# Four of eight conditioning shifts summed along rows on VectorE instead of multiplied on TensorE

## The chip, the cores and the metric

The kernel runs on one core of a Trainium2 chip, as one launch. The metric is the device time of that launch in microseconds (us). A core has a matrix engine (TensorE, PE in the profile; PEld is its weight load), a vector engine (VectorE, DVE), an activation engine (ScalarE, ACT), GpSimd (POOL) and SyncE (SP), which here only issues transfers. Each engine works through its own queue in order. DMA transfers are issued from SP's queue (nearly all) and from ScalarE's.

## The reference

Two layers of a diffusion backbone over 256 latent tokens and 256 context tokens, 2048 channels wide. Layer 0 is attention plus a state-space mixer, layer 1 a gated short convolution. What matters here is how layer 0 gets its input: a conditioning vector makes a shift, a scale and a gate, and the normalised tokens are scaled and shifted by them, the latent ones with `c`, the context ones with `c_ctx`.

```python
def adaln(cond, w, b):
    m = jax.nn.silu(cond) @ w + b
    return jnp.split(m, 3, axis=-1)

def modulate(h, shift, scale):
    return h * (1 + scale) + shift

shift, scale, gate = adaln(c, ada_w[i], ada_b[i])
h = modulate(rms_norm(x, norm_g[i]), shift[:, None], scale[:, None])
shift_c, scale_c, gate_c = adaln(c_ctx, ada_w[i], ada_b[i])
hc = modulate(rms_norm(ctx, norm_g[i]), shift_c, scale_c)
p = h @ w_in                    # w_in: 2048 x 14400
pc = hc @ w_in[:, base:]
```

`ada_w[0]` is 2048 x 6144 in fp32: 16 MB each for shift, scale and gate. Every weight is read once, and it meets two condition vectors (shift and scale) or one (gate).

## The kernel before

**The schedule.** The kernel is written out by a planner. `Plan` holds a clock for each engine, a table of when each piece of a tile is written, and a clock for the DMA engines, which advances by bytes over `RATE` (270 GB/s). Work besides the main loop sits in generators ("tasks") in three lists, `urgent`, `side` and `back`. A task yields what its next step needs: an engine and tiles, or a condition. `pump` runs every step that by the planner's clocks would find its engine and its tiles ready within a horizon (4500 ns for `urgent`, 2500 for `side`, 1500 for `back`, `HOR`), so the clocks decide the order of instructions on each engine's queue. `force(ok, qs)` runs the best step of the lists `qs` again and again until `ok` holds; the main loop calls it before it writes work that needs a result.

**Loads.** `loads` is one list of transfers in a fixed order, most of them 512 KB in a buffer of 128 x 1024 fp32. There are nine such buffers in this stage (`raw` 0 to 4, and four tiles used later, which the profile shows as `PT`, `xtm` and `yi`). `issue` (L381, L383) takes the next transfer whenever a buffer is free; a user gives its buffer back with `give_raw`. A weight is split into a high and a low part, a cast on ScalarE (L420) and a subtraction on VectorE (L427), into one of three places, and every product is made of three: high by high, high by low, low by high.

**Layer 0's first stage** goes over the 2048 channels in eight blocks j of 256. For each block and each of four token tiles `kv` multiplies with the key and the value weights, for two tiles with the query weights, and `b_part` makes a part of the B projection. Key and value parts of a block go to a bank each and are added up by VectorE (`part_gen`, L789), which frees the bank. A block needs its modulated tokens, split into `hH` and `hL`. The main loop says so:

```python
for j in range(8):
    need[0] = j
    force(lambda: ("h", j, 0 if j == 0 else 3) in got, (urgent,))
```

They come from `ada_gen`, one task that takes the blocks in order. For a block it makes the scale `A0` (part 0), then the shift `S0` (part 1), each from four loads of `ada0`: 16 products of 128 x 32 with the padded condition vectors `cpad` as weights, a copy on ScalarE (L724), two transposes, a short reduction on VectorE (L732) and one or two short additions (L735 to L738). Then for each of the two channel blocks of 128 it computes `hH` on ScalarE (L757, two activations), the same in full fp32 on VectorE (L759, two operations), and the difference `hL` on VectorE (L763). The load order is, for block j: its key and value weights, scale and shift loads of block j+1 (`q_ada`), its query weights, its B weights.

**The gate** of layer 0 and all of layer 1's conditioning are computed by `gemv_gen` in the list `back`: the SiLU of `c` is written to memory as a row (`crow`, by `rows_out`), half a row is loaded to all partitions (`csb`), and each load of transposed weights is multiplied by it and summed along the row in one VectorE operation (L823). Nothing needs these before the output projection of layer 0. In the first stage it runs beside the last blocks.

Of the kernel before, what the change touches and what calls it, by code (L numbers as in the profile page):

```python
# [14 lines left out]
D = 2048  # L15
KB = 16
# [125 lines left out]
def kernel(ctx: ExitStack, tc, x, cx, ada0, w0, adaT, w_in, w_out, sc_in, sc_out, rpb, small, const,  # L142
# [216 lines left out]
    onload = {}  # L359

    later = deque()
    started = [False]
    ngem = [0]

# [120 lines left out]
    def q_ada(j, *parts):  # L485
        for part in range(2):
            if parts and part not in parts:
                continue
            for q in range(4):
                loads.append(("a", ("ada", j, part, q), ada0, 8 * j + 4 * part + q, 4, 0, 256, 2))  # L490

    def q_proj(w, c0, nc_, rows=D):
        room[0] = 2 if w is w_in and c0 >= COL_K else 1
# [208 lines left out]
    def ada_gen():  # L702
        bc = lambda ap: ap.unsqueeze(2).to_broadcast([128, 2, 2])
        for j in range(8):
            k2 = slice(2 * j, 2 * j + 2)
            for part, dst in ((0, A0), (1, S0)):
                ps = None
                for q in range(4):
                    key = ("ada", j, part, q)
# [31 lines left out]
            for ts in ((0, 1), (2,), (3,)) if j == 0 else ((0, 1, 2, 3),):  # L741
                yield when(lambda: all(("xm", t, j) in got for t in ts))
                spans = [(k, slice(max(256 * k, 128 * ts[0]), min(256 * k + 256, 128 * ts[-1] + 128)))
                         for k in range(2) if {2 * k, 2 * k + 1} & set(ts)]
                o = slice(128 * ts[0], 128 * ts[-1] + 128)
                for kb in (2 * j, 2 * j + 1):
                    if j:

                        yield when(lambda: need[0] >= j or plan.t["DVE"] <= plan.t["PE"] + 600)
                    yield W_("DVE", xnT[kb][:, o])  # L750
                    hf = tmp()
                    if hH[kb] is None:
                        hH[kb] = st([128, 512], f"hH{kb}", F32R, name=f"hH{kb}")
                    if ts == (0, 1):
                        split_half(kb)
                    for k, ok_ in spans:
                        E(S.activation(hH[kb][:, ok_], xnT[kb][:, ok_], AF.Identity, scale=A0[:, kb, k:k + 1],  # L757
                                       bias=S0[:, kb, k:k + 1]))
                        E(V.tensor_scalar(out=hf[:, ok_], in0=xnT[kb][:, ok_], scalar1=A0[:, kb, k:k + 1],  # L759
                                          scalar2=S0[:, kb, k:k + 1], op0=ALU.mult, op1=ALU.add))  # L760
# [30 lines left out]
        got.add(("part", j, key, t))  # L791


    mrow, crow = drt([2, D], "mrow"), drt([1, D], "crow")
# [6 lines left out]
    def rows_out(col, dst):  # L801

        yield W_("PE", col, nb=1)
        ps = bank()
        turn(ps[:16, :128], col)
        yield W_("DVE", ps)
        E(V.tensor_copy(rowt[:16, :], ps[:16, :128]))
        give(free_b, ps)
        yield W_("AQ", rowt)
        E(DMA2.dma_start(dst.rearrange("(b c) -> b c", c=128), rowt[:16, :]))  # L810

    def gemv_gen():
        yield from rows_out(csil[:, 0:KB], crow[0])
        for q, blocks in enumerate(GEM):
            for h in range(2):
                yield W_("SP", crow, csb)
# [12 lines left out]
            if q == 1:  # L829
                a, b = p2(16, 32)  # L830
                o = M1.rearrange("p r b -> p (r b)")
                E(V.tensor_tensor(out=o, in0=a, in1=b, op=ALU.add))
                E(V.tensor_tensor(out=o, in0=o, in1=P_("ab1")[:, 0:32], op=ALU.add))
            else:
                a, b = p2(0 if q == 0 else 48, 16)
                E(V.tensor_tensor(out=a, in0=a, in1=b, op=ALU.add))
                E(V.tensor_tensor(out=a, in0=a, in1=P_("ab0" if q == 0 else "ab1")[:, 32:48], op=ALU.add))
                yield from rows_out(a, mrow[q // 2])
            n_back[0] = (3, 11.5, 15)[q]

    spawn(back, gemv_gen())
# [27 lines left out]

    for j in range(8):  # L870
        need[0] = j
        force(lambda: ("h", j, 0 if j == 0 else 3) in got, (urgent,))
        if j == 0:

            w3 = [use(k) for k in range(3)]
# [27 lines left out]
        else:  # L903
# [1209 lines left out]
```

## Time and profile before

| | |
|---|---|
| median of 3 runs | 1753.41 us (1752.1 to 1754.06) |
| the profiled execution, its own time | 1752.57 us |
| its span, first to last instruction | 1750.8 us |
| busy: TensorE, VectorE, ScalarE | 1730.9, 1218.1, 768.5 us |
| first stage, blocks 1 to 7 | 51.4 to 194 us of the span |

The profile is of one execution. A window or timeline counts from the first instruction. Busy times of one engine can overlap by some hundredths of a microsecond at the ends of instructions. "L427" is line 427 of the kernel; helpers record many operations on one line (L195 is every product, L199 every transpose). After `<-` stands what ended an idle time.

### The profile page before, as it was taken

The page shows a single profiled execution, that of the slowest core. Times are in us where ns is not written, and L with a number is a line of the kernel's source. Part 1 is how long each engine was busy: PE and PEld are TensorE (multiplying, and loading weights), DVE is VectorE, ACT ScalarE, POOL GpSimd, SP SyncE. Part 2 cuts the span into 40 slices and gives each one's busy share as a digit, 9 for nine tenths or more (in the row PEclk, how much of TensorE's full clock was granted, in tenths as well). Part 3 has the DMA queues.
Part 4 walks back from the last instruction along what each step waited for, and adds up shares of the span by engine and source line. Part 5 has one row for each costly group of instructions (what it writes and reads, how often), then busy time and mean ns, then how long its engine had stood idle before and what let it go on. Part 6 is the DMA issues. An engine that isn't in the chain of part 4 may idle for free.

```text
span 1750.8 us, 25076 instructions
## 1 busy us (share of the span) xinstructions
PE 1730.9 (99%) x9451; PEld 1461.3 (83%) x9451; DVE 1218.1 (70%) x2042; ACT 768.5 (44%) x1330; POOL 33.2 (2%) x28
## 2 busy tenths in 40 slices
PE   6999999999999999999999999999999999999998
PEld 4777988889888889888888898888888888888887
DVE  5666787868575877675877687887568766555554
ACT  5333544446243435243435243655445444444432
POOL 0000100001000000000001000000000000000000
PEclk9999999999999999999999999999999999999999
DMA  9987644776655766665766667867867878666563
GB/s 368 345 303 259 192 144 121 207 230 203 218 175 150 220 212 183 203 190 163 221 217 183 185 196 248 261 213 260 279 206 253 266 239 257 188 192 193 192 211 114
DMA packets 193369, 378.98 MB, mean 216 GB/s; under 512 B 18096, under 2 KB 57824, under 8 KB 193248
## 3 DMA queue, kind: packets, MB, share of 16 engines
q1 hardware_dynamic: 185984, 370.80, 66.2%
q10 hardware_dynamic: 7264, 6.58, 1.2%
q8 instruction: 74, 1.21, 0.3%
q14 instruction: 47, 0.39, 0.1%
HBM read 369.83 MB, written 7.50 MB: 216 GB/s over the span
## 4 chain that ended last, share of the span: by engine, by line
PE 98%; DMA 0%; DVE 0%; SPq 0%; ACT 0%; issue 0%; POOL 0%; DVEq 0%; ACTq 0%
PE bank L195 95%; PE bank L199 3%; DMA raw<-in_ada 0%; SPq L583 0%; DVE w L427 0%; DVE tmp L603 0%; DVE tmp L759 0%; ACT half L724 0%; ACT x L613 0%; DVE tmp L2016 0%; DVE tmp L2018 0%; DVE hL L763 0%; SPq L381 0%; ACT hH L757 0%; DVE gt L789 0%
## 5 line engine op out<-in xcount | busy, mean ns | idle before, releaser
L427 DVE TENSOR_TENSOR w<-raw,w 128x1024 fp32r<-128x1024 f32 x343 | 416.4, 1217 | 260.6 <-ACT w L420 254.7
L420 ACT CAST w<-raw 128x1024 fp32r<-128x1024 f32 x343 | 359.2, 1049 | 531.2 <-PE bank L195 454.5
L195 PE MATMUL bank<-hH,w 128*128 128x256 f32 (+1 forms) x2064 | 486.5, 324 | 0.0
L195 PE MATMUL bank<-w,hH 128*128 128x512 f32 x1280 | 406.5, 396 | 2.7 <-ACT hH L757 2.5
L195 PEld LDWEIGHTS bank<-hH,w 128*128 128x128 f32 x2064 | 344.7, 188 | 32.0 <-issue 1.7
L195 PE MATMUL bank<-hL,w 128*128 128x256 f32 (+1 forms) x1040 | 334.5, 322 | 0.0
L195 PEld LDWEIGHTS bank<-w,hH 128*128 128x128 f32 x1280 | 236.8, 188 | 54.1 <-issue 4.2
L195 PE MATMUL bank<-w,hL 128*128 128x512 f32 x640 | 249.4, 390 | 0.1
L195 PEld LDWEIGHTS bank<-hL,w 128*128 128x128 f32 x1040 | 196.3, 189 | 14.4
L195 PE MATMUL bank<-w,h 128*128 128x512 f32 x768 | 179.7, 390 | 0.0
L195 PEld LDWEIGHTS bank<-w,h 128*128 128x128 f32 x768 | 143.6, 188 | 29.6
L823 DVE CUSTOM_DVE_ANT_0 raw<-raw,csb 128x1024 f32<-128x1024 f32 x128 | 155.2, 1218 | 11.9 <-DMA raw<-in_adaT 10.0
L195 PEld LDWEIGHTS bank<-w,hL 128*128 128x128 f32 x640 | 120.1, 188 | 25.4 <-DVE hL L763 0.6
L195 PE MATMUL bank<-w,mix 128*128 128x512 f32 x588 | 139.1, 392 | 0.0
L195 PEld LDWEIGHTS bank<-w,mix 128*128 128x128 f32 x588 | 109.1, 188 | 22.4 <-DVE w L427 0.3
L1279 DVE SCALAR_TENSOR_TENSOR tmp<-bank,cwh,tmp 128x508 f32<-128x508 f32 (+1 forms) x96 | 71.1, 745 | 1.9
L195 PE MATMUL bank<-KL,h 128*128 128x512 f32 x264 | 63.9, 389 | 0.0
L427 DVE TENSOR_TENSOR QL<-raw,QT 128x1024 fp32r<-128x1024 f32 x32 | 39.2, 1224 | 29.0 <-ACT QT L420 28.9
L427 DVE TENSOR_TENSOR KL<-raw,KL 128x1024 fp32r<-128x1024 f32 x32 | 39.2, 1224 | 28.4 <-ACT KL L420 28.3
L195 PEld LDWEIGHTS bank<-KL,h 128*128 128x128 f32 x264 | 49.5, 188 | 10.3
L427 DVE TENSOR_TENSOR wL<-raw,wH 128x1024 fp32r<-128x1024 f32 x31 | 37.9, 1224 | 27.4 <-ACT wH L420 27.4
L195 PE MATMUL bank<-QT,h 128*128 128x512 f32 x168 | 56.2, 391 | 0.0
(293 smaller groups left out, 1975.0 us busy)
## 6 DMA issues: line engine op xcount, KB each, us to landing
raw<-in_w_in SPq DMA_DIRECT2D x196, 512.0 KB, 3.8
raw<-in_adaT SPq DMA_DIRECT2D x128, 512.0 KB, 4.7
raw<-in_sc_in SPq DMA_DIRECT2D x128, 512.0 KB, 3.9
raw<-in_w_out SPq DMA_DIRECT2D x64, 512.0 KB, 5.2
raw<-in_ada SPq DMA_DIRECT2D x34, 512.0 KB, 6.8
raw<-in_sc_out SPq DMA_DIRECT2D x32, 512.0 KB, 3.6
PT<-in_ada SPq DMA_DIRECT2D x16, 512.0 KB, 6.9
raw<-in_w SPq DMA_DIRECT2D x16, 512.0 KB, 6.5
```

Of the source, the lines that this page charges most:

```text
L195: E(T.matmul(o, l, r, start=start, stop=stop, skip_group_check=True))
L199: E(T.transpose(o, i, ident if k == 128 else ident[:k, :k]))
L420: E(S.copy(H, v))
L427: E(V.tensor_tensor(out=Lo, in0=v, in1=H.bitcast(F32), op=ALU.subtract))
L823: E(V.tensor_tensor_reduce(out=raw, in0=raw, in1=csb, scale=1.0, scalar=0.0, op0=ALU.mult, op1=ALU.add, accum_out=gp[:, h, m:m + 1]))
L1279: E(V.scalar_tensor_tensor(out=do, in0=di, scalar=cwh[:, 32 * k + ch:32 * k + ch + 1], in1=do, op0=ALU.mult, op1=ALU.add))
```

## The change

For blocks 4 to 7 (`DOTS`) the shift is not multiplied on TensorE. The weights of these shifts are laid out transposed by the host, so that an output channel is a partition and 1024 of the 2048 inputs are a row; the number and size of the loads stay. Both conditions are written to memory as rows (`crow` has two), and a new task `dot_gen` in the list `side` loads each whole row to all 128 partitions, into the tiles `KT` and `KL`, which are free once the tokens are transposed. For every load it issues two VectorE operations that multiply by a condition row and sum along it, one for each condition, then the short reduction and the addition of the bias. `ada_gen` skips the shift of these blocks and waits for it instead. The main loop forces `side` tasks as well as `urgent` ones from block 1 on.

These loads stand beside the scale loads of the same block, two ahead of them and two behind, in the stretch of the load order that belongs to the block before.

The full-fp32 modulated tokens of blocks 1 to 7 are computed on ScalarE (two more activations behind L757's) instead of VectorE. `gemv_gen` starts its loads of `csb` after the last of the new sums, which use `csb` for results that nobody reads. From block 1 to the end of the stage the planner's DMA clock runs at 360 GB/s instead of 270.

```diff
+    DOTS = (4, 5, 6, 7)
@@ q_ada
             for q in range(4):
-                loads.append(("a", ("ada", j, part, q), ada0, 8 * j + 4 * part + q, 4, 0, 256, 2))
+                if part and j in DOTS:
+                    loads.append(("a", ("dot", j, q), ada0, 8 * j + 4 + q, 1, 0, 1024, 2))
+                else:
+                    loads.append(("a", ("ada", j, part, q), ada0, 8 * j + 4 * part + q, 4, 0, 256, 2))
@@ the order of loads
+    dots = deque()
+
+    def dot_load():
+        for _ in range(2):
+            if dots:
+                loads.append(dots.popleft())
+
     for j in range(1, 8):
+        for jj in DOTS:
+            if j == max(1, jj - 1):
+                q_ada(jj, 1)
+                for _ in range(4):
+                    dots.append(loads.pop())
+                dots = deque(sorted(dots, key=lambda a: a[1][1:]))
         w_seg(j, CK, CV)
+        dot_load()
         if j < 7:
-            q_ada(j + 1)
+            q_ada(j + 1, *((0,) if j + 1 in DOTS else (0, 1)))
+        dot_load()
         w_seg(j, CQ)
         weight(w_in, j * 256, 2, COL_B, 256)
@@ ada_gen
             for part, dst in ((0, A0), (1, S0)):
+                if part and j in DOTS:
+                    yield when(lambda: ("S", j) in got)
+                    continue
...
-                    yield W_("DVE", xnT[kb][:, o])
+                    yield W_("ACT" if j else "DVE", xnT[kb][:, o])
...
+                        if j:
+                            E(S.activation(hf[:, ok_], xnT[kb][:, ok_], AF.Identity, scale=A0[:, kb, k:k + 1],
+                                           bias=S0[:, kb, k:k + 1]))
+                            continue
                         E(V.tensor_scalar(out=hf[:, ok_], in0=xnT[kb][:, ok_], scalar1=A0[:, kb, k:k + 1],
                                           scalar2=S0[:, kb, k:k + 1], op0=ALU.mult, op1=ALU.add))
+                    if j:
+                        yield W_("DVE", hf)
@@ the new task
+    def dot_gen():
+
+        yield when(lambda: "crow" in got and all(("xm", t, 7) in got for t in (2, 3)) and need[0] >= 2)
+        full = []
+        for c in range(2):
+            yield W_("SP", crow)
+            full.append(st([128, D], ("KT", "KL")[c], name=f"full{c}"))
+            E(DMA.dma_start(full[c], crow[c].partition_broadcast(128)))
+        part_ = statk.rearrange("p (b c h) -> p b c h", b=4, c=2)
+        for j in DOTS:
+            for q in range(4):
+                yield when(lambda: ("dot", j, q) in RAW)
+                raw = RAW["dot", j, q][0]
+                for c, o in enumerate((csb, raw)):
+                    yield W_("DVE", raw, full[c])
+                    E(V.tensor_tensor_reduce(out=o, in0=raw, in1=full[c][:, (q % 2) * 1024:(q % 2) * 1024 + 1024], scale=1.0,
+                                             scalar=0.0, op0=ALU.mult, op1=ALU.add,
+                                             accum_out=part_[:, q // 2, c, q % 2:q % 2 + 1]))
+                RAW.pop(("dot", j, q))
+                give_raw(raw)
+                issue()
+            k2 = slice(2 * j, 2 * j + 2)
+            yield W_("DVE", statk)
+            S_ = S0[:, k2, :]
+            E(V.tensor_reduce(out=S_, in_=part_[:, 0:2], axis=AX.X, op=ALU.add))
+            E(V.tensor_tensor(out=S_, in0=S_, in1=P_("ab0")[:, k2].unsqueeze(2).to_broadcast([128, 2, 2]), op=ALU.add))
+            got.add(("S", j))
@@ gemv_gen
-        yield from rows_out(csil[:, 0:KB], crow[0])
+        yield from rows_out(csil, crow.rearrange("r (b c) -> (r b) c", c=128), 32)
+        got.add("crow")
+        yield when(lambda: ("S", DOTS[-1]) in got)
@@ the main loop
     spawn(urgent, x_gen(1), 1)
+    spawn(side, dot_gen())
...
         need[0] = j
-        force(lambda: ("h", j, 0 if j == 0 else 3) in got, (urgent,))
+        if j == 1:
+            plan.RATE = 360.0
+        force(lambda: ("h", j, 0 if j == 0 else 3) in got, (urgent,) if j == 0 else (urgent, side))
...
     force(lambda: all(("part", 7, key, t) in got for key in "KV" for t in range(4)), (urgent,))
+    plan.RATE = Plan.RATE
@@ on the host
+    for j in (4, 5, 6, 7):
+        for q in range(4):
+            k0, c0 = (q % 2) * 1024, j * 256 + (q // 2) * 128
+            ada0[8 * j + 4 + q] = f('ada_w')[0][k0:k0 + 1024, c0:c0 + 128].T
```

More of the change, by code (lines that the diff above doesn't have):

```diff
@@ L791, in part_gen @@
         got.add(("part", j, key, t))
-    mrow, crow = drt([2, D], "mrow"), drt([1, D], "crow")
+    mrow, crow = drt([2, D], "mrow"), drt([2, D], "crow")
     M1 = st([128, 2, KB], "M1")
@@ L799, with rows_out @@
     n_back = [0]
-    def rows_out(col, dst):
+    def rows_out(col, dst, n=16):
         yield W_("PE", col, nb=1)
         ps = bank()
-        turn(ps[:16, :128], col)
+        turn(ps[:n, :128], col)
         yield W_("DVE", ps)
-        E(V.tensor_copy(rowt[:16, :], ps[:16, :128]))
+        E(V.tensor_copy(rowt[:n, :], ps[:n, :128]))
         give(free_b, ps)
         yield W_("AQ", rowt)
-        E(DMA2.dma_start(dst.rearrange("(b c) -> b c", c=128), rowt[:16, :]))
+        E(DMA2.dma_start(dst, rowt[:n, :]))
+    in_rows = lambda r: r.rearrange("(b c) -> b c", c=128)
+    def dot_gen():
[24 more added lines that the diff above has]
+            got.add(("S", j))
     def gemv_gen():
-        yield from rows_out(csil[:, 0:KB], crow[0])
+        yield from rows_out(csil, crow.rearrange("r (b c) -> (r b) c", c=128), 32)
+        got.add("crow")
+        yield when(lambda: ("S", DOTS[-1]) in got)
         for q, blocks in enumerate(GEM):
@@ L837, in gemv_gen @@
                 E(V.tensor_tensor(out=a, in0=a, in1=P_("ab0" if q == 0 else "ab1")[:, 32:48], op=ALU.add))
-                yield from rows_out(a, mrow[q // 2])
+                yield from rows_out(a, in_rows(mrow[q // 2]))
             n_back[0] = (3, 11.5, 15)[q]
```

## The prediction

> **What bounds the kernel now.** I read the page first, for what the span is made of.
>
> ```profile
> span 1750.8 us, 25076 instructions
> PE 1730.9 (99%) x9451; PEld 1461.3 (83%) x9451; DVE 1218.1 (70%) x2042; ACT 768.5 (44%) x1330; POOL 33.2 (2%) x28
> PE 98%; DMA 0%; DVE 0%; SPq 0%; ACT 0%; issue 0%; POOL 0%; DVEq 0%; ACTq 0%
> ```
>
> TensorE is busy for 1730.9 of 1750.8 us, and the chain that ended last is TensorE for 98%. So time leaves this kernel only where TensorE gets less to do, and it comes back wherever TensorE is made to wait. The profiled execution took 1752.57 us, 1.77 more than its span; the median of the runs, 1753.41, is 0.84 above that.
>
> Next the windows, cut at the borders of layer 0's first stage. Block 1 starts at 51.4 us, block 2 at 72.3, block 7 at 177.7; its rows end at 194. The columns are the window, its length, busy us (count) of PE, weight load, DVE, ACT and POOL, granted clock, DMA share, GB/s.
>
> ```profile
> 0.00:44.00 44.00, 29.10 (x235) 19.36 (x236) 24.86 (x75) 26.03 (x59) 3.19 (x10) 1.00 0.95 368
> 44.00:51.40 7.40, 7.40 (x40) 5.83 (x38) 6.45 (x15) 6.58 (x15) 0.00 (x0) 1.00 1.03 416
> 51.40:72.30 20.90, 20.90 (x142) 15.77 (x142) 13.13 (x24) 6.62 (x11) 0.00 (x0) 1.00 0.96 355
> 72.30:177.70 105.40, 105.22 (x702) 77.83 (x701) 65.48 (x120) 32.25 (x51) 0.00 (x0) 1.00 0.76 276
> 177.70:194.00 16.30, 16.30 (x73) 13.51 (x72) 11.87 (x17) 3.76 (x5) 0.00 (x0) 1.00 0.50 161
> 194.00:1750.80 1556.80, 1551.95 (x8267) 1328.98 (x8265) 1096.33 (x1795) 693.29 (x1194) 29.99 (x18) 1.00 0.66 206
> ```
>
> From 44 to 194 us TensorE loses 0.18 us in all, with the clock full. VectorE is 62% busy (65.48 of 105.40) where the change puts its sums, ScalarE 31%. The DMA engines are full up to 72 us and then 0.76.
>
> **What is taken from TensorE.** The shift of one block is 16 products, whose 32 records stand as one piece in the timeline, and two transposes. Start, length, engine, operation, tiles, count:
>
> ```profile
> 59.52 0.39 PE L195 MATMUL bank<-w,hH 128*128 128x512 f32 x1
> 59.84 1.93 PE L195 MATMUL bank<-raw,cpad 128*32 128x256 f32 x32
> 61.70 0.50 PE L195 MATMUL bank<-w,hH 128*128 128x512 f32 x1
> 62.04 0.40 PE L195 MATMUL bank<-w,hL 128*128 128x512 f32 x1
> 62.27 0.39 PE L195 MATMUL bank<-w,hH 128*128 128x512 f32 x1
> 62.50 0.38 PE L199 MATMUL bank<-const,half 128*128 128x128 f32 x2
> 62.64 0.48 PE L195 MATMUL bank<-w,hH 128*128 128x512 f32 x1
> 62.95 0.40 PE L195 MATMUL bank<-w,hL 128*128 128x512 f32 x1
> ```
>
> Undisturbed row products start 0.23 us apart (62.04 to 62.27). From the start at 59.52 to that at 62.95 are 3.43 us, in which five row products start; at 0.23 they take 1.15. So one shift costs 2.28 us, the slow starts behind each change of tile shape included. Four shifts are 9.1 us, and no wait covers them, so all of it is on the path: **minus 9.1**.
>
> **What VectorE gets.** Operations by shape between 72.3 and 177.7 us, and three starts in a row:
>
> ```profile
> L427 DVE TENSOR_TENSOR w<-raw,w 128x1024 fp32r<-128x1024 f32 x10 | 12.2, 1223 | 3.5 <-ACT w L420 3.4
> L759 DVE TENSOR_SCALAR tmp<-xm,A,S 128x256 f32<-128x256 f32 x21 | 7.7, 406 | 0.0
> L823 DVE CUSTOM_DVE_ANT_0 raw<-raw,csb 128x1024 f32<-128x1024 f32 x2 | 2.4, 1216 | 0.0
> 169.90 1.22 DVE L823 CUSTOM_DVE_ANT_0 raw<-raw,csb 128x1024 f32<-128x1024 f32 x1
> 171.04 0.08 DVE L823 DVE_READ_ACCUMULATOR2_ANT gp<- 128x1 f32 x1
> 171.04 1.27 DVE L789 TENSOR_TENSOR Vt<-Vt,bank 128x512 f32<-128x512 f32 x2
> ```
>
> The trace has the added operation itself: L823 is the same sum along a row, 1.216 us, with 1.14 to the next start, so its accumulator read costs nothing more. The change adds 4 blocks by 4 loads by 2 sums, 32 of them: 38.9 us by duration, 36.5 by starts. It takes away the L759 group (7.7 us), which goes to ScalarE; the short reductions and additions behind each shift stay as many. Between 72.3 us and block 7, VectorE then has 65.5 − 7.7 + 38.9 = 96.7 us of busy time in 105.4 − 9.1 = 96.3. Busy times overlap by 0.08 each (169.90 + 1.22 against 171.04); over some 131 instructions that is 10, so the need is between 86 and 97 us: 90 to 100%. Nor can the sums begin at 72.3: they wait for the two whole condition rows and a first load, 12 to 16 us by the transfers and landings below; I take 14. In the 82 us left, the rest of VectorE's work is 57.8 × 82/96.3 = 49, together 88 by durations and 79 by starts. Behind a late sum on VectorE's queue stand the additions that free banks and the low halves of weights, and TensorE waits for both. So this costs from nothing to 6 us. I take **plus 2.5**, nearer the lower end because starts, not durations, are what an engine's queue keeps.
>
> [...]
>
> The slack is in when the shift is needed:
>
> ```profile
> 161.59 0.17 DVE L732 TENSOR_REDUCE S<-bank 128x4 f32<-128x16 f32 x1 [2.96 <-PE bank L199]
> 177.69 0.39 PE L195 MATMUL bank<-w,hH 128*128 128x512 f32 x1
> ```
>
> Block 7's shift is ready at 161.59 and its rows start at 177.69. A sum may slip by some 10 us, and what follows it still fits. Without that cover each late block costs what the second rival works out.
>
> **What ScalarE gets.** ScalarE's queue just before block 1:
>
> ```profile
> 45.44 1.10 ACT L757 ACTIVATE hH<-xm,S,A 128x256 fp32r<-128x256 f32 x2 [0.82 <-DVE S L738]
> 48.22 1.11 ACT L757 ACTIVATE hH<-xm,S,A 128x256 fp32r<-128x256 f32 x2
> 49.22 2.00 ACT L420 CAST w<-raw 128x1024 fp32r<-128x1024 f32 x2
> ```
>
> From block 1 on, each of two channel blocks has two more activations there, 1.1 us (1.10 for two), so 2.2 us a block. From 72.3 on that lies beside an engine at 31%, and nothing waits for it. But between 44 and 51.4 ScalarE is busy for 6.58 of 7.40 us, and 2.2 more make 8.8. Behind them stand the casts of block 1's weights. The excess is 1.4 us, less what VectorE gains by losing L759, and the later order may hide it: from nothing to 2.2. I take **plus 1.0**.
>
> **What the DMA gets.** Issues with their median us to landing, and the bytes from 51 to 178 us:
>
> ```profile
> DMA packets 11717, 36.70 MB, mean 289 GB/s; under 512 B 1182, under 2 KB 2974, under 8 KB 11707
> raw<-in_ada SPq DMA_DIRECT2D x22, 512.0 KB, 6.2
> csb<-dram_crow SPq DMA_DIRECT2D x1, 512.0 KB, 10.1
> 74.20 0.90 SPq L381 DMA_DIRECT2D raw<-in_w  x2
> 88.33 1.05 ACT L420 CAST w<-raw 128x1024 fp32r<-128x1024 f32 x1 [3.70 <-issue]
> ```
>
> The shift's loads keep their bytes and their number. New are two broadcasts of a whole condition row, 128 × 8 KB each, 2.1 MB, put on SP's queue at block 2; the 512 KB one of before moves behind the stage. At the 355 to 416 GB/s of the full windows, 2.1 MB are 5 to 6 us of all engines, and the loads behind them on SP's queue come that much later. With a landing of 6 to 10 us behind them, the first sum stands 12 to 16 us into block 2. Over the stage, 38.8 MB in 126.3 − 9.1 = 117 us is 331 GB/s, under what the full windows moved. The price goes from nothing to 5.6, if none of the delay is covered; but block 3's key weights, issued at 74.20, are cast at 88.33 only, 8 us after a landing of 6.2, so **plus 0.5**. The planner's 360 GB/s is within the 355 to 416 delivered, so an order made for it makes products wait little, and it returns buffers sooner than one made for 270. The gate's sums (L823) wait until block 7's shift is done; their first was at 169.90, and that shift comes earlier, so nothing.
>
> **After the stage** the planner's clock differs, and with it the order of what follows. TensorE is idle there for 4.85 of 1556.80 us, which is all there is to win; as much may be lost. I take 0, with 2 either way.
>
> **Sum:** −9.1 + 2.5 + 1.0 + 0.5 = −5.1: 1747.5 against the profiled 1752.57, and **1748.3** against the median.
>
> **Rivals.** First, full gain: the sums fit into gaps and block 1 hides the activations. For it: 16 us of lead, DVE at 62%. Against it: the 90 to 100%. 1753.4 − 9.1 = 1744.3.
>
> Second, slower: sums come out of the planner only when a block can't start without them. The scaling generator takes its blocks in order, so block j+1's scale products wait behind block j's sums, and unsummed loads keep the nine buffers from the weights. Then the chain behind the last sum stands between blocks: reduction and addition 0.3 us, eight activations 4.4, one low half 0.7, less the first products that can start on half of it: 5.0 us. It decides when the lead of 16 us is used up, that is when VectorE needs over 100% for three blocks on end. At blocks 5, 6 and 7 it is 15: −9.1 + 15 + 1.0 gives 1760. For it: the need by durations, and buffers that are held longer. Against it: the need by starts.
>
> Third, a draw: VectorE sets the pace and costs 6, with 2.2 at block 1: 1752.5, within what can't be told apart. (A measurement of this kernel can tell about 0.2%, 3.5 us, from no change.)
>
> [...]
>
> That the four shifts leave TensorE isn't in doubt; that the planned rate does anything may be, and is inside the 2 us of order.
>
> **How the numbers follow.** Forecast 0.50, with a range of its own from 1744.3 (no price) to 1751.5 (4, 2.2 and 1.0): 0.42 of it faster than 1749.9, 0.08 the same. Full gain 0.12, faster. Draw 0.14, same. Late sums 0.22, slower; double cost 0.02, slower. Faster 0.54, same 0.22, slower 0.24. For 8 in 10: down to 1742.5, which is full gain and most of the 2 us of order, up to 1760, which leaves out the upper half of the slow case, double cost and a little below.
>
> **What would show it.** Right: 128 of the 512 condition products' records (32 for each scale and each shift of eight blocks) are gone, with two transposes for each shift; block 7's rows end near 189 instead of 194; 32 more L823-like operations near 1.22 us; VectorE over 85% busy from 85 to 165 us; TensorE's idle time between 44 and 190 at 2 to 5 us, behind additions, low halves or L420 casts, part of it near 51 us. Wrong: sums near 2.4 us; TensorE waiting at the start of blocks 5 to 7 for hH or hL; a wait for loads between 72 and 100 us; or a difference that arises after 194 us.

## The result, and the profile after

The changed kernel takes 1756.92 us (median; 1755.64 to 1761.3) against 1752.79 us: ratio 1.0024, 95% interval 1.0015 to 1.0033. It is 4.1 us slower; the forecast was 5.1 faster. The profiled execution is the slowest of its eight, at 1761.3 us, so its account explains 8.7 us of span, not 4.1. Executions of one kernel differ by several us: those of the kernel before, in all comparisons here, took 1751.74 to 1758.08 us, and its profiled one, 1752.57, is near the low end.

The page, with its totals and its chain:

```profile
span 1759.5 us, 24836 instructions
PE 1729.1 (98%) x9315; PEld 1460.3 (83%) x9315; DVE 1244.4 (71%) x2078; ACT 781.2 (44%) x1354; POOL 33.3 (2%) x28
PE 87%; DMA 2%; ACT 1%; DVE 1%; issue 0%; SPq 0%; ACTq 0%
```

TensorE has 136 instructions fewer: the 128 records of the products and the 8 transposes of four shifts. But its busy time fell by 1.8 us instead of 9.1, its idle time rose from 19.9 to 30.4 us, and the chain is TensorE for 87% instead of 98%.

The same windows as before:

```profile
44.00:51.40 7.40, 6.48 (x43) 4.92 (x36) 3.29 (x9) 6.26 (x16) 0.00 (x0) 1.00 1.02 402
51.40:72.30 20.90, 20.90 (x158) 14.77 (x160) 13.12 (x21) 10.20 (x18) 0.00 (x0) 1.00 0.86 324
72.30:177.70 105.40, 99.87 (x562) 76.14 (x554) 93.20 (x160) 41.83 (x67) 0.00 (x0) 0.99 0.83 303
177.70:194.00 16.30, 15.98 (x59) 12.44 (x59) 10.22 (x15) 2.49 (x5) 0.00 (x0) 0.83 0.29 103
194.00:1759.50 1565.50, 1556.67 (x8279) 1332.44 (x8277) 1099.73 (x1798) 694.83 (x1195) 30.15 (x18) 1.00 0.64 205
```

From 44 to 194 us TensorE idles 6.8 us (0.18 before), and after 194 us 8.8 (4.85 before). The granted clock (TensorE's clock as the profile shows it, 1.00 is full) was 1.00 in every window before and is 0.83 in the fourth.

One event marks the end of the stage in every kernel, ScalarE's first cast into `KT`: before, then after.

```profile
208.78 1.07 ACT L1014 CAST KT<-bank 128x512 fp32r<-128x512 f32 x2 [1.66 <-PE bank L199]
```

```profile
211.50 1.07 ACT L1078 CAST KT<-bank 128x512 fp32r<-128x512 f32 x2 [1.66 <-PE bank L199]
```

So the stage is 2.7 us longer instead of 8.2 shorter (the 9.1 less the 0.9 at block 1), and 6.0 more arise behind it.

**Inside the stage.** TensorE's waits in the timeline:

```profile
49.51 0.50 PE L195 MATMUL bank<-hH,w 128*128 128x512 f32 x1 [0.39 <-ACT w L421]
50.78 0.74 PE L195 MATMUL bank<-hH,w 128*128 128x512 f32 x2 [0.53 <-DVE w L428]
155.84 0.50 PE L195 MATMUL bank<-w,hL 128*128 128x512 f32 x1 [1.46 <-DVE hL L791]
157.16 0.44 PE L199 MATMUL bank<-const,half 128*128 128x128 f32 x2 [0.58 <-ACT half L746]
175.12 0.50 PE L195 MATMUL bank<-w,hH 128*128 128x512 f32 x1 [1.80 <-ACT hH L779]
177.32 0.79 PE L195 MATMUL bank<-w,hL 128*128 128x512 f32 x1 [1.70 <-DVE hL L791]
179.28 0.79 PE L195 MATMUL bank<-w,hL 128*128 128x512 f32 x1 [0.32 <-DVE hL L791]
```

0.9 us stand before block 1, 2.0 at the start of block 6, 3.8 at block 7. They wait for tokens, and the tokens wait for VectorE. Its window from the first sum on, its commonest sums there, and the short reductions that end the shifts of blocks 4 to 7:

```profile
89.70:175.00 85.30, 81.59 (x450) 62.44 (x448) 82.44 (x142) 31.83 (x49) 0.00 (x0) 1.00 0.79 286
```

```profile
L857 DVE CUSTOM_DVE_ANT_0 raw<-raw,full 128x1024 f32<-128x1024 f32 x9 | 11.0, 1220 | 0.1
L857 DVE CUSTOM_DVE_ANT_0 csb<-raw,full 128x1024 f32<-128x1024 f32 x9 | 11.0, 1220 | 0.3 <-DMA full<-dram_crow 0.3
```

```profile
107.69 0.16 DVE L866 TENSOR_REDUCE S<-statk 128x4 f32<-128x8 f32 x1
129.01 0.15 DVE L866 TENSOR_REDUCE S<-statk 128x4 f32<-128x8 f32 x1
152.42 0.15 DVE L866 TENSOR_REDUCE S<-statk 128x4 f32<-128x8 f32 x1
174.07 0.16 DVE L866 TENSOR_REDUCE S<-statk 128x4 f32<-128x8 f32 x1
```

A sum takes 1.220 us as forecast, but VectorE is busy for 82.44 of 85.30 us and delivers a shift every 21 to 23 us. The stage before needed 21.1 us for a block (105.40 / 5), so TensorE without the shift's 2.28 needs 18.8. Block 7's shift, ready 16 us ahead before, ends at 174.07, when TensorE has been standing at that block since 173.3.

The granted clock falls behind the waits at block 7. The same stretch in steps of 4 us, then cut where the clock changes:

```profile
176.00:180.00 4.00, 2.36 (x5) 1.45 (x6) 1.38 (x2) 2.50 (x6) 0.00 (x0) 0.57 0.84 315
180.00:184.00 4.00, 4.00 (x12) 3.12 (x11) 2.52 (x4) 0.00 (x0) 0.00 (x0) 0.58 0.16 47
```

```profile
176.60:180.00 3.40, 2.36 (x5) 1.45 (x6) 1.35 (x2) 1.91 (x4) 0.00 (x0) 0.50 0.80 302
180.00:183.40 3.40, 3.40 (x10) 2.63 (x9) 2.13 (x4) 0.00 (x0) 0.00 (x0) 0.51 0.04 10
```

For 6.8 us the clock is half (0.50 and 0.51), and products there start 0.43 us apart (180.73 to 181.16), against 0.23 once it is back (184.02 to 184.25). TensorE is busy for 5.76 us of them (the rest is already counted as waits), so this costs some 2.9 us, an estimate. The stage's account is then −9.1 + 0.9 + 5.9 + 2.9 = +0.6; measured is +2.7, and 2.1 of it I cannot assign. 1.2 us of that are missing in e3_none too (third group), which has no sums: its stage is 7.0 us shorter than before, not 8.2.

**Behind the stage** nearly all of the 6.0 us arises near 400 us. SP's queue, TensorE's wait, and the clock there (`csb` is a half row of the condition for the gate, issued right behind four loads into `tmp`):

```profile
383.99 2.00 SPq L1499 DMA_DIRECT2D tmp<-dram_csr  x4
386.36 0.35 SPq L382 DMA_DIRECT2D raw<-in_adaT  x1
386.75 3.47 SPq L877 DMA_DIRECT2D csb<-dram_crow  x1
401.66 1.01 PE L195 MATMUL bank<-tmp,xtm 128*64 128x128 f32 x6 [3.72 <-DVE tmp L1528]
```

```profile
400.00:404.00 4.00, 2.34 (x9) 1.78 (x10) 3.90 (x11) 2.70 (x7) 0.00 (x0) 0.73 0.45 133
404.00:408.00 4.00, 4.00 (x16) 3.26 (x15) 3.25 (x9) 0.83 (x2) 0.00 (x0) 0.85 0.76 218
```

3.72 us of waiting and 1.7 at a low clock (an estimate, 4 × 0.27 + 4 × 0.15). Before, TensorE had no wait there: it was busy for all 40.00 us from 380 to 420.

### The profile page after: what moved, and what is told of

The parts are those of the page before. It is cut to its first block, busy times and chain, and to the rows that moved or that the text cites. A ratio compares the mean times of both kernels' runs of the same rounds, so it can differ in the third digit from the quotient of the medians.

```text
span 1759.5 us, 24836 instructions
## 1 busy us (share of the span) xinstructions
PE 1729.1 (98%) x9315; PEld 1460.3 (83%) x9315; DVE 1244.4 (71%) x2078; ACT 781.2 (44%) x1354; POOL 33.3 (2%) x28
## 4 chain that ended last, share of the span: by engine, by line
PE 87%; DMA 2%; ACT 1%; DVE 1%; issue 0%; SPq 0%; ACTq 0%
PE bank L195 84%; PE bank L199 3%; DMA tmp<-dram_csr 1%; DMA tmp<-dram_mixd 1%; DMA raw<-in_w_out 0%; ACT w L421 0%; DVE w L428 0%; ACT tmp L1508 0%; ACT tmp L782 0%; ACT hH L779 0%; DVE tmp L1523 0%; SPq L1499 0%; DVE tmp L1528 0%; ACT tmp L1518 0%; ACT mix L1678 0%
## 5 line engine op out<-in xcount | busy, mean ns | idle before, releaser
L428 DVE TENSOR_TENSOR w<-raw,w 128x1024 fp32r<-128x1024 f32 x344 | 416.9, 1215 | 263.1 <-ACT w L421 261.4
L428 DVE TENSOR_TENSOR QL<-raw,QT 128x1024 fp32r<-128x1024 f32 x32 | 39.2, 1224 | 29.5 <-ACT QT L421 29.5
L428 DVE TENSOR_TENSOR KL<-raw,KL 128x1024 fp32r<-128x1024 f32 x32 | 39.2, 1224 | 28.5 <-ACT KL L421 28.4
L428 DVE TENSOR_TENSOR wL<-raw,wH 128x1024 fp32r<-128x1024 f32 x31 | 37.9, 1224 | 27.7 <-ACT wH L421 27.7
```

The costliest lines, as they stand in the source:

```text
L428: E(V.tensor_tensor(out=Lo, in0=v, in1=H.bitcast(F32), op=ALU.subtract))
```

## The experiments

"Stage" is how much later than before the first cast into `KT` starts, "end" how much longer the span is; both are of one profiled execution, the ratio is of all executions of a run against those of the kernel before beside it. One execution can be several us off its kernel's median (e3_free_gate's is the fastest of ten, from 1755.77 to 1763.93 us; e4_pool's the slowest of ten, from 1751.98 to 1758.92), so small differences in the last two columns show nothing by themselves.

| run | ratio (95%) | stage | end |
|---|---|---|---|
| the change | 1.0024 (1.0015 to 1.0033) | +2.7 | +8.7 |
| e1_half | 0.9998 (0.9986 to 1.0010) | +2.4 | +3.8 |
| e1_two | 1.0039 (1.0024 to 1.0054) | +4.4 | +9.4 |
| e1_rate270 | 1.0030 (1.0016 to 1.0044) | +4.1 | +6.3 |
| e1_rate_only | 1.0011 (1.0000 to 1.0022) | +1.4 | +2.0 |
| e2_hf_dve | 1.0041 (1.0026 to 1.0056) | +7.7 | +8.3 |
| e2_act_only | 1.0009 (1.0000 to 1.0019) | +1.2 | +2.9 |
| e2_early | 1.0065 (1.0048 to 1.0082) | +7.6 | +9.5 |
| e2_two_dve | 1.0054 (1.0039 to 1.0068) | +7.9 | +12.2 |
| e3_none | 0.9949 (0.9934 to 0.9964) | −7.0 | −6.9 |
| e3_loads | 1.0034 (1.0023 to 1.0045) | −3.5 | +5.6 |
| e3_free | 1.0026 (1.0015 to 1.0036) | +5.9 | +6.4 |
| e3_free_gate | 1.0036 (1.0024 to 1.0048) | +0.9 | +3.2 |
| e4_gate | 1.0034 (1.0020 to 1.0047) | +7.9 | +9.1 |
| e4_pool | 1.0006 (0.9993 to 1.0018) | −3.9 | +6.3 |
| e4_nocsb | 1.0013 (1.0003 to 1.0023) | +2.2 | +6.6 |
| e4_best | 1.0034 (1.0021 to 1.0047) | +7.9 | +12.3 |
| e5_half_late | 0.9960 (0.9947 to 0.9973) | −6.5 | −6.2 |
| e5_two_late | 0.9992 (0.9980 to 1.0004) | −2.1 | −0.9 |

**First: room, rate, or chain.** Theory 1: VectorE has no room. Theory 2: the order written for 360 GB/s costs. Theory 3: the longer row of activations on ScalarE costs.

```diff
 e1_half: one sum for each load instead of two (and statk is zeroed first)
-                for c, o in enumerate((csb, raw)):
+                for c, o in enumerate((csb,)):
 e1_two (and the host's layout for these two blocks alone)
-    DOTS = (4, 5, 6, 7)
+    DOTS = (6, 7)
 e1_rate270
-            plan.RATE = 360.0
+            plan.RATE = 270.0
 e1_rate_only: the kernel before, with the planner at 360 GB/s from block 1 to the stage's end
+        if j == 1:
+            plan.RATE = 360.0
```

e1_half: 

> Leaves out the second sum of every load (the context tokens' shift is then the bias alone): 16 sums instead of 32, everything else as in the changed kernel. Theory 1 (VectorE has no room: it runs without a gap from 89.7 to 175 us, so the last two shifts are late, and TensorE waits some 5.6 us and then runs for a while at a lower granted clock): the need falls by 19 us, no shift is late, TensorE idles under 1 us between 140 and 180, and the time is 1743 to 1747. Theory 2 (the order made for 360 GB/s is what costs, within the stage and behind it): 1755 to 1758, as before the cut. Theory 3 (the eight activations between a shift and its rows, now all on ScalarE, are the wait): 1750 to 1756, with TensorE still waiting for hH and hL at the starts of blocks 6 and 7.

e1_two: 

> Only blocks 6 and 7 have their shift summed on VectorE. Theory 1: VectorE needs about 77 of 101 us between 72 and 178 and nothing is late; two shifts leave TensorE (4.6 us), about 1.5 us go at the start of the stage: 1749 to 1751. Theory 2: 1755 to 1758, since the rate is the same. Theory 3: 1755 to 1757, with waits for hH and hL at blocks 6 and 7.

e1_rate270: 

> The changed kernel with the planner's rate left at 270 GB/s. Theory 1: the sums are as many, so the time stays within 3 us of the changed kernel's, 1755 to 1760. Theory 2: the loss goes, 1747 to 1751. Theory 3: as theory 1.

e1_rate_only: 

> The kernel of before with only the planner's rate for the stage set to 360 GB/s. Theory 1: same time as before within 2 us, 1751 to 1755. Theory 2: slower by 3 to 6 us, 1756 to 1759. Theory 3: as theory 1.

The planned rate is not the main cause: taking it back changes nothing that can be told apart, and alone it costs 1.9 us (0.0 to 3.9), with two waits of TensorE for loads of the scale (0.58 and 0.43 us). Nor does fill alone explain it: leaving out half of the sums brings back 4.6 us (by the ratios) of the 12 missing, and sums for two blocks alone are no better than for four. By its time e1_half fits Theory 3 as well; the second group takes that up. In both of these TensorE still waits. For the longest wait in e1_half the timeline shows for what. VectorE, then TensorE:

```profile
121.28 1.23 DVE L859 CUSTOM_DVE_ANT_0 csb<-raw,full 128x1024 f32<-128x1024 f32 x1 [1.12 <-DMA raw<-in_ada]
124.95 1.28 DVE L817 TENSOR_TENSOR sz<-sz,bank 128x512 f32<-128x512 f32 x2
125.77 0.55 PE L195 MATMUL bank<-w,hH 128*128 128x512 f32 x1 [2.14 <-DVE sz L817]
```

A sum stands at the head of VectorE's queue for its load for 1.12 us. Behind it come another sum and a low half, and only then, at 124.95, the addition that frees a bank, for which TensorE waits 2.14 us. In e1_two a low half of weights comes too late in the same way:

```profile
118.34 1.23 DVE L857 CUSTOM_DVE_ANT_0 csb<-PT,full 128x1024 f32<-128x1024 f32 x1 [3.87 <-DMA PT<-in_ada]
121.23 1.22 DVE L428 TENSOR_TENSOR w<-xtm,w 128x1024 fp32r<-128x1024 f32 x1
122.51 0.73 PE L195 MATMUL bank<-w,hH 128*128 128x512 f32 x2 [1.48 <-DVE w L428]
```

That is 1.48 of the 6.0 us that TensorE idles in e1_two from 85 to 190 us; the shorter waits are not traced to a load.

**Second: the parts of the edit.** The tokens' full-fp32 operations go back to VectorE (e2_hf_dve). The same operations go to ScalarE in the kernel before, and nothing else changes (e2_act_only). The sums may start at block 1 (e2_early). Sums for blocks 6 and 7 alone, with 270 GB/s and the operations on VectorE (e2_two_dve).

```diff
 e2_hf_dve
-                    yield W_("ACT" if j else "DVE", xnT[kb][:, o])
+                    yield W_("DVE", xnT[kb][:, o])
 ...
 e2_early
-        yield when(lambda: "crow" in got and all(("xm", t, 7) in got for t in (2, 3)) and need[0] >= 2)
+        yield when(lambda: "crow" in got and all(("xm", t, 7) in got for t in (2, 3)) and need[0] >= 1)
```

e2_hf_dve: 

> The changed kernel with the full-fp32 modulated tokens back on VectorE; sums and rate stay. Theory 3 (the longer chain of activations): VectorE's waits for them (8.7 us in the changed kernel) fall under 3, TensorE's loss of 0.9 us near 50 us goes, and with it most of the waits at blocks 6 and 7: 1749 to 1753. Theory 1 (no room on VectorE): 8 us more work in a full stretch, 1759 to 1764.

e2_act_only: 

> The kernel of before with only those operations moved to ScalarE. Theory 3: 0.9 us near 50 us and short waits for hL at the block starts, 1754 to 1757. Theory 1: no other loss than the 0.9 us: 1752.5 to 1754.5.

e2_early: 

> The changed kernel with the condition rows and the sums let go one block earlier (from block 1 instead of 2). Theory 1: the first sum comes near 75 instead of 89.7 us, the shifts of blocks 6 and 7 are ready some 10 us earlier, the waits of 5.6 us between 150 and 180 us go: 1747 to 1751. Theory 3: the waits at the block starts stay, 1755 to 1758. A third cost would be the rows' 2.1 MB in a stretch in which the DMA engines are full: a wait for loads near 60 to 75 us of up to 5 us.

e2_two_dve: 

> The kernel of before with sums for blocks 6 and 7 alone: no move to ScalarE, rate 270 GB/s. Theories 1 and 3: VectorE has room, the chain is the old one, and the old rate places the sums behind their landings; two shifts are 4.6 us: 1748.5 to 1751. Theory 2 in its other form (any new order costs some 3 us in this stage): 1752 to 1756.

ScalarE's part alone costs 1.6 us (0.0 to 3.3), with waits of 0.37 and 0.53 us before block 1, as in the changed kernel. More work on VectorE (e2_hf_dve) makes the stage 5 us longer, as Theory 1 has it; by Theory 3 the time would have fallen to 1749 to 1753, so that is not the main cause. e2_early tells nothing of an earlier start: its first sum began at 90.09 us, no earlier than 89.70. Why it is the slowest of all stays open.

e2_two_dve, at 1762.37 us, is slower than any of the theories allowed. No sum in it waits for a load, and VectorE is busy for only 79.82 of the 105 us from 85 to 190, yet TensorE idles 8.0 us there, mostly for hL. Near 138 us, VectorE, then TensorE:

```profile
136.39 1.21 DVE L851 CUSTOM_DVE_ANT_0 yi<-yi,full 128x1024 f32<-128x1024 f32 x1
137.53 0.73 DVE L781 TENSOR_SCALAR tmp<-xm,A,S 128x256 f32<-128x256 f32 x2
138.36 0.69 DVE L785 TENSOR_TENSOR hL<-tmp,hH 128x512 fp32r<-128x512 f32 x1
139.11 0.50 PE L195 MATMUL bank<-w,hL 128*128 128x512 f32 x1 [1.67 <-DVE hL L785]
```

A sum stands just ahead of the tokens that TensorE needs next. So the place of a sum in the queue can cost with room to spare and without waiting for a load.

**Third: a ladder from nothing to everything.** Without loads and sums of the four shifts (e3_none); with the loads, each read by a copy of one column on VectorE (e3_loads); with all loads and sums, their results not waited for (e3_free); and that with the rule changed by which `ada_gen` hands out a block's tokens (e3_free_gate). In all four the shift of blocks 4 to 7 is the bias alone.

```diff
 e3_loads, in place of the two sums; e3_none has neither this nor the loads
-                for c, o in enumerate((csb, raw)):
 ...
+                yield W_("DVE", raw)
+                E(V.tensor_copy(statk[:, 4 * (q // 2) + q % 2:4 * (q // 2) + q % 2 + 1], raw[:, 0:1]))
 all four, at block 2
+            E(V.tensor_copy(S0[:, k2, :], P_("ab0")[:, k2].unsqueeze(2).to_broadcast([128, 2, 2])))
+            got.add(("S", j))
 e3_free_gate
-                        yield when(lambda: need[0] >= j or plan.t["DVE"] <= plan.t["PE"] + 600)
+                        yield when(lambda: need[0] >= j or plan.t["DVE"] <= plan.t["PE"] + 4000)
```

e3_none: 

> The changed kernel with the shift of blocks 4 to 7 left out altogether: no loads of it, no whole condition rows, no sums; the shift of those blocks is the bias alone, written once at block 2. ScalarE's part and the planned rate stay. It tells whether the 9.1 us are there to be had. If they are (the sum's first term holds): minus 9.1, and about plus 1 of block 1, so 1744 to 1747 against 1753.4, with TensorE idle under 1.5 us from 44 to 190 us. If the slow order after the stage or something else in the edit costs by itself: 1750 to 1756, with the stage shorter by 8 and the time lost behind it.

e3_loads: 

> As the run before, but the 16 loads of the four shifts are issued and held as in the changed kernel, and VectorE copies one column of each (about 0.1 us) where two sums of 1.22 us stood; no whole condition rows. If the sums' time on VectorE is the cost (theory of room or of the queue): within 1.5 us of the run without loads. If buffers and transfers of the loads cost (theory of loads): 3 us or more above it, with TensorE waiting for weights (w) or VectorE's queue standing at a load.

e3_free: 

> The changed kernel with all its loads, rows and 32 sums, but nobody waits for their results: the shift of blocks 4 to 7 is the bias alone, written at block 2. If the chain behind a late sum (second rival: sum, reduction, activations, low half) is the cost: 5 us or more below the changed kernel's 1757, so under 1752, with no waits for hH or hL at the starts of blocks 5 to 7. If VectorE's room is the cost, whoever waits: within 2.5 us of 1757, with VectorE busy without a gap and TensorE waiting for hL, sz or w all the same.

e3_free_gate: 

> As the run before, and the rule that hands out a block's tokens before the block starts (VectorE's planned clock at most 0.6 us ahead of TensorE's) loosened to 4 us. If it is this rule that puts the tokens at the last moment, because the sums keep VectorE's planned clock 2 to 3 us ahead: 3 us or more below the run before, waits for hL at block starts gone. If VectorE has no room, the waits only move to sz, gt and w, and the time is within 2 us of the run before.

The saving is there: 1745.37 us, 8.2 below by medians (7.0 in the profiled stage), with TensorE at 105.40 of 105.40 us:

```profile
72.30:177.70 105.40, 105.40 (x602) 82.09 (x595) 65.89 (x106) 43.48 (x69) 0.00 (x0) 1.00 0.63 220
```

e3_free is no faster than the changed kernel, though nobody waits for a sum. It still has waits for tokens at block 7, 1.41 us for hH and 1.70 for hL: their shift is known from block 2 on, but they are handed out at the block's start, since VectorE is planned ahead of TensorE. With the rule loosened (e3_free_gate) those waits are gone, and TensorE waits for banks instead, up to 2.37 us behind VectorE's additions into `sz` and `gt`; by its median that is no faster either. So with all 32 sums it is not the lateness of a sum's result that costs, it is VectorE's queue, and TensorE meets it in one place or the other.

e3_loads surprised me: no sums at all, and 1759.45 us. Its stage is 3.5 us shorter than before, 3.5 less than e3_none's gain; TensorE waits there for two loads of the scale (0.79 and 0.85 us) and once for a bank (0.91). And it loses 9.1 us behind the stage, nearly half of it here (TensorE, then the clock):

```profile
1115.81 4.38 PE L195 MATMUL bank<-w,mix 128*128 128x512 f32 x11 [2.68 <-DVE Vt L1101]
```

```profile
1116.00:1120.00 4.00, 4.00 (x11) 3.12 (x11) 4.00 (x9) 2.03 (x4) 0.00 (x0) 0.57 0.34 95
```

The instructions there are those of the kernel before; only their order and the transfers beside them differ. A kernel without any sum is thus as slow in all as the changed one, so what the sums cost is read from the stage alone: −7.0 us without loads and sums, −3.5 with the loads, +2.7 with both.

**Fourth: three causes, one by one.** The tokens' rule alone in the changed kernel (e4_gate, the same line as above); the one-column copies on the idle GpSimd (e4_pool); the gate's second half row left out (e4_nocsb); the rule together with the tokens of block 1 as before (e4_best).

```diff
 e4_pool, against e3_loads
-                yield W_("DVE", raw)
-                E(V.tensor_copy(statk[
+                yield W_("POOL", raw)
+                E(G.tensor_copy(statk[
 e4_nocsb
+                if (q, h) != (0, 1):
                     E(DMA.dma_start(csb, crow[0, h * 1024:(h + 1) * 1024].partition_broadcast(128)))
```

e4_gate: 

> The changed kernel with one number changed: a block's tokens may be handed out while VectorE's planned clock is up to 4 us ahead of TensorE's, instead of 0.6. If the hand-out at the last moment (the second rival's chain, brought about by this rule) is the cost: 3 to 6 us below the changed kernel, so 1751 to 1754, with no waits for hL at block starts and the granted clock at 1.00. If the sums are late anyway, because VectorE has no room: within 2 us of 1757.

e4_pool: 

> The run with the 16 loads and no sums, its one-column copies moved from VectorE to the idle GpSimd; shift of blocks 4 to 7 is the bias alone. If the loads cost because VectorE's queue stands at them (17 us of such waits in that run) with additions behind it: the stage gets 2 to 3 us shorter, to within 1.5 of the run without loads. If it is transfers or buffers: the stage is the same, and TensorE waits for the scale's loads (raw<-in_ada) as before.

e4_nocsb: 

> The changed kernel without the second of the six broadcasts of half the condition row for the gate (its sums use the first half's values), the one that was issued at 386.75 us right behind four small loads of 256 KB. If this broadcast delays those loads: the wait of 3.7 us near 402 us and the low clock behind it are gone, the difference from before stays at the stage's 2.9 us instead of 8.5, and the slow executions of the changed kernel (1760 to 1761) with them: 1754 to 1757. If not: 1757, and the wait is there.

e4_best: 

> The changed kernel with the 4 us rule, and with the second activation of the tokens on ScalarE only from block 2 on (block 1 as before the change). If the parts add up: 0.9 us below the run with the rule alone, TensorE without waits near 50 us; 1750 to 1753, at best level with the kernel before. If VectorE's room decides: no better than the run with the rule alone.

The rule is no cause: the stage gets 5 us longer, and block 7's shift comes later still:

```profile
177.58 0.16 DVE L866 TENSOR_REDUCE S<-statk 128x4 f32<-128x8 f32 x1
```

With 32 sums, tokens handed out earlier only push sums back: VectorE is busy for 56.0 of the 60 us from 100 to 160. e4_pool's stage is 0.4 us shorter than e3_loads', not 2 to 3; with no sums to queue behind, the short copies were nearly harmless (the wait of 0.91 us for a bank is gone), though they stood 17 us at the head of VectorE's queue for their loads. So what the loads cost in the stage is likely their transfer or their buffer: TensorE waits there for four loads of the scale, 0.62, 0.67, 0.20 and 0.63 us. Its ratio is 0.0028 (4.9 us) lower all the same; where that arises the two profiles do not show, as e4_pool's is the slowest of its ten executions and e3_loads' the fastest of its seven. e4_nocsb still waits 2.82 us at 400 us, so that broadcast is not the cause of the wait there. e4_best is no better than e4_gate. TensorE still waits 0.37 and 0.74 us near 50 us, although block 1's tokens are made as before: under the loosened rule four activations for hH stand in one piece (46.50 to 48.58 us) ahead of the cast of weights that comes at 49.27.

**Fifth: the queue's head.** A sum is handed out only when its load is planned to have landed 5 us before, or when its block starts, in two runs in which VectorE has room (e1_half and e1_two). e5_half_late leaves out half of the sums, as e1_half does; e5_two_late leaves out nothing.

```diff
                 raw = RAW["dot", j, q][0]
+                yield when(lambda: need[0] >= j or plan.ready([raw]) + 5000 <= plan.t["DVE"])
```

e5_half_late: 

> The run with one sum a load instead of two (half of the shift's sums left out), and each sum is put on VectorE's queue only when its load is planned to have landed 5 us before (or its block starts). If sums standing at the queue's head for their loads are the cost: no wait of VectorE over 0.5 us at a sum, TensorE's waits between 60 and 190 us under 3 us instead of 5.4, and 3 us or more below the run without the rule (1752.9 against 1754.3 then), so a ratio of 0.998 or less. If it is the load's transfer and the buffer that it holds: no better, since buffers are held longer, ratio 1.000 or more, with TensorE waiting for weights or scale loads.

e5_two_late: 

> The same rule on the run with the sums of blocks 6 and 7 alone (two sums a load, nothing left out). If the queue's head is the cost: 3 to 5 us below that run's ratio of 1.0039, so 1.001 to 1.002, with the wait of 1.5 us for w near 122 us gone. If VectorE's whole load or the transfers are: 1.003 or more.

One line brings 6.7 us with half of the sums and 8.2 with those of two blocks, by the ratios. VectorE's sums in e1_half, then in e5_half_late, with the window of each:

```profile
L859 DVE CUSTOM_DVE_ANT_0 csb<-raw,full 128x1024 f32<-128x1024 f32 x7 | 8.6, 1223 | 4.0 <-DMA raw<-in_ada 3.6 <-DMA full<-dram_crow 0.3
```

```profile
89.70:175.00 85.30, 79.88 (x429) 60.71 (x428) 64.77 (x111) 32.47 (x53) 0.00 (x0) 0.96 0.85 302
```

```profile
L860 DVE CUSTOM_DVE_ANT_0 csb<-raw,full 128x1024 f32<-128x1024 f32 x7 | 8.6, 1222 | 0.3 <-DMA full<-dram_crow 0.2
```

```profile
89.70:175.00 85.30, 84.71 (x469) 66.10 (x468) 71.26 (x119) 35.15 (x55) 0.00 (x0) 1.00 0.86 315
```

The waits for loads are gone, TensorE idles 0.6 us instead of 5.4 in this window, and the clock is 1.00 instead of 0.96. That handing the sums out too early cost these two runs their gain is shown, with one reservation: the order of other instructions changes with it. That they cost by standing for their loads is only likely: the rule also moves sums out of the way of what stands behind them when no load is awaited, and e2_two_dve loses more with no such wait. e5_two_late, 1751.61 us, is the fastest that leaves nothing out, and it cannot be told from the kernel before.

## Why the prediction was wrong

**Minus 9.1** held in kind: 9.1 less 0.9 at block 1 is 8.2, and e3_none gives 8.2 by medians, 8.9 by its ratio (6.3 to 11.6) and 7.0 in its profiled stage. That one of them agrees to the tenth is luck; by the stage a shift is worth some 2.0 us instead of 2.28.

**Plus 1.0 at block 1** held: 0.92 us of waits, 1.6 (0.0 to 3.3) when done alone.

**A sum's price** held: 1.220 us with its result in `csb` and 1.220 with it in `raw`, where the plain subtraction of the same shape (L428) took 1.223. The double cost to which the prediction gave 0.02 is shown by no run: the groups of sums in the traces average 1.214 to 1.227 us.

**Plus 2.5 for VectorE's fill** is the step that failed. The prediction had a need of 88 us by durations and 79 by starts in 82, and took the low end. Measured, the sums and what lay between them took 84.4 us (89.70 to 174.07) with VectorE full: more than the 82, and more, block by block, than TensorE's 18.8. The sums also began at 89.70, 17.4 us behind 72.3, where 12 to 16 were forecast. The other half of the error was to price the fill as an average over the stage. VectorE's queue delivered the shifts 21.3, 23.4 and 21.7 us apart, so the lead of 16 us was used up, and all the waiting came at the last two blocks. In place of 2.5 stand 5.9 us of waits.

**The granted clock** was in no term. It cost some 2.9 us in the stage and 1.7 near 400 us (the estimates above), more than the largest cost that I had entered.

**The DMA's 0.5** looked for a wait of TensorE for loads and found none; right for the changed kernel, where VectorE is so far behind that only the first sum waits. What it missed is that a load can hold VectorE's queue instead, as in the rows of e1_half and e1_two, and that the loads cost by themselves: 3.5 us in the stage of e3_loads, with no sums. How much of this is in the changed kernel's +2.7 is not shown.

**0 after the stage, 2 either way** was wrong in its symmetry. I wrote that TensorE's 4.85 us of idle time were all there was to win and as much might be lost. In the table, the end's difference less the stage's is what arises behind the stage: between 0.1 us (e3_none) and 10.2 (e4_pool). That none is below zero proves less than it seems, since all are measured against one fast execution of the kernel before; by medians the changed kernel's 4.1 us less 2.7 leave 1.4. But the larger ones are waits and low clocks in the traces, and no trace shows a gain to match. What decides their size is open: e4_nocsb took away the neighbour that I suspected, and the wait stayed.

**The second rival** (1760, chance 0.22) came nearest in time, with waits at block starts and the lead used up, as it said. But its cause was the late sum, and e3_free, where nobody waits for a sum, is as slow. Its 15 us at three blocks were 5.9 at two; that 1760 came near is luck, as the clock and the order behind the stage, in none of its terms, made up for part of the rest. So the sign and the place were its own; what stood behind them was VectorE's queue. Of the signs that I had named, the two for wrong came true that fitted it, waits for hH and hL at block starts and a difference behind 194 us.

Not tried: the 5 us rule on all four blocks. There only the first sum waits for a transfer, so by these traces the rule has little to take away; room would have to come first.

## What to carry to other kernels

Before work is moved to an engine that feeds the bottleneck, compare its need with the time between two deadlines, not with the whole stage, and take the durations' end when the two ends straddle the limit. Look also at what stands behind an operation that nobody needs yet. On VectorE's queue here a sum just ahead of the next tokens left TensorE waiting 1.67 us for them (e2_two_dve), and one that stood 1.12 us for its own load was followed by a wait of 2.14 us for a bank (e1_half); in two runs, handing the sums out some us after the planned landing brought back 6.7 and 8.2 us. And a schedule almost without waits has little to win when it is written anew (4.85 us of TensorE's idle time here) and more to lose: lay the range for "the order behind it" to the slow side.

## What the runs showed of the hardware

Behind some short waits the granted clock fell, and there a wait cost more than its length. In the changed kernel it is 0.50 to 0.51 for 6.8 us behind the waits at block 7 (rows above); near 400 us it is 0.50 from 402.0 to 405.2 us. Two waits of 1.46 and 0.59 us within 2 us were followed by 4 us at 0.57 (e2_early); one of 2.37 us was followed by none (e3_free_gate). The waits and the windows behind them, of the one and of the other:

```profile
137.81 0.50 PE L195 MATMUL bank<-w,hL 128*128 128x512 f32 x1 [1.46 <-DVE hL L791]
139.13 0.44 PE L199 MATMUL bank<-const,half 128*128 128x128 f32 x2 [0.59 <-ACT half L746]
```

```profile
140.00:144.00 4.00, 4.00 (x12) 3.13 (x11) 3.54 (x7) 0.64 (x1) 0.00 (x0) 0.57 0.98 321
```

```profile
171.66 0.50 PE L195 MATMUL bank<-w,hH 128*128 128x512 f32 x1 [2.37 <-DVE gt L817]
```

```profile
172.00:176.00 4.00, 4.00 (x19) 3.31 (x18) 4.00 (x8) 1.21 (x2) 0.00 (x0) 1.00 0.08 28
```

The same two waits, 1.46 and 0.58 us, stood in the changed kernel at 155.84 and 157.16, and the clock stayed at 1.00 from 156 to 164 us. Where a drop came it cost 1.7 us (4 us at 0.57) to 2.9 (estimates). The longest wait just ahead of a drop was 1.46 us in e2_early, 1.80 at block 7, 2.68 in e3_loads and 3.72 near 400 us; waits of 1.46 and 2.37 us came without one. By these traces a wait's length alone does not tell whether the clock falls, so a term for it, with a chance, belongs in the sum as soon as waits like these are expected.
